# Low parts of the weights: GpSimd's columns moved to VectorE, in a two-block network on one core

## The chip, the cores and the metric

One core of a Trainium2 chip runs the whole program. The metric is the device time of one execution in microseconds (us). TensorE's matrix rows are called PE here, its weight loads PEld, VectorE DVE, ScalarE ACT, GpSimd POOL, and the engine that issues the transfers SP.

## The reference

A sequence of 256 positions with 1024 channels goes through two blocks, each two layers deep. Cut to what matters:

```
first block, twice:   x += 0.5 * swiglu(rms(x), w_gu, w_down)          # 1024 -> 2*2816 -> 1024
                      x += hybrid_mixer(rms(x))     # gMLP branch, attention over selected keys, gates
                      x += 0.5 * swiglu(rms(x), ...)
x = rms(x)
second block, twice:  x += rms(hybrid_mixer_2(rms(x)))   # gated delta rule, dilated attention
                      x += rms(conv_glu_ffn(rms(x)))     # 1024 -> 2*2816, 3-tap conv, gelu*val, -> 1024
```

All of it is float32. Nearly all arithmetic is products of activations with weight matrices.

## The kernel before

TensorE reads its operands in a reduced float32 form (`R32`), so each float32 operand is cut into a high part (`hi`) and a low part (`lo = value - hi`), and each product is made of three matmuls: hi*hi, lo*hi and hi*lo (`mm3_steps`, L254 to L273).

The activations are cut once per stage. The weights come as pieces of mostly 128 x 1024 numbers (512 KB), and each piece is cut when it is needed: SP loads it into a `wraw` buffer (4 of them), ACT copies it to `whi` (4 buffers, the copy's line is L185), and a subtraction makes `wlo` (4 buffers, line L202 whatever the engine). A `wraw` buffer comes free when both copies are made, `whi` and `wlo` when TensorE has read them. This is `parts` (L233), called by `piece`.

The subtraction is divided by columns: VectorE takes the first ones, GpSimd the last `pool_cols`, which is 384 of a piece (640 for VectorE of a piece of 1024, 384 of 768, 128 of 512). In the mixer of the second block a list `plan` gives a number of its own per piece: there `FULL = 34` of the pieces go to GpSimd whole, the four pieces ahead of them half and half. The first piece of the program goes to VectorE whole.

The stages in their order in time: feed-forward 1 to 205 us, mixer 1 to 380, feed-forward to 580, the same three again to 1155, then the second block: mixer 2 (1155 to 1364), gated feed-forward `conv_glu` (to 1580), and both again (mixer 2 to 1785, `conv_glu` to the end). Feed-forward stages run over 22 pairs of pieces (up projection), then over 8 output chunks of three pieces (down projection).

One step of `conv_glu`'s up projection, for one of 22 pairs: two pieces give 48 matmuls; VectorE multiplies the result by the norm row (`t`), ACT and VectorE run the three-tap convolution (`y`: one ACT instruction and two VectorE ones for each half), ACT applies the gelu (`s`), VectorE multiplies (`p`), ACT rounds it to the high part of `hid`, GpSimd makes the low part of `hid`.

In mixer 2 the delta rule is a long dependent chain of small operations. Its start is `rates` on VectorE: from `bt` over `xa`, `spe`, `spz` and `sps` to `dg`, with the convolution of the keys (`kT`) woven in by hand. The order on TensorE is written by hand there too: `pump` puts a fixed amount of other matmuls (pieces of the input projection) where TensorE would wait for the chain.

The order of the instructions of each engine is otherwise set by a scheduler when the program is built, from its own model of their durations; each engine then runs its list strictly in order.

Of the kernel before, what the change touches and what calls it, by code (L numbers as in the profile page):

```python
# [10 lines left out]
OP = mybir.AluOpType  # L11
# [8 lines left out]
D = 1024  # L20
# [5 lines left out]
NEG = -1.0e30  # L26
TAKEN = -3.0e38
BANKS = {"mm": 3, "sm": 5}
FIRST_COLS = 384
POOL_COLS = 384  # L30
FULL = 34
X_ENG = ((ACT, ACT), (ACT, ACT))
XT_ENG = ((ACT, ACT), (ACT, ACT))
WARM = (0, 5, 3)
# [56 lines left out]
class Kernel:  # L91
# [9 lines left out]
    def run(self, stages=None):  # L101
        nc, I, cp = self.nc, self.I, self.cp
        stages = stages or STAGES
        first = [s for s in stages if s[0] not in ("final", "mixer2", "glu")]
        vec1 = self.load(cp, [P, 8 + 2 * V1], I["vec1"], "vec1")
        self.x, self.ahead = [], []
        self.before = self.latest = self.ready = self.later = None
        self.plan, self.made, self.queue, self.far = [], [], [], 0
        self.pool_cols = FIRST_COLS
        for d in range(KD):  # L110
            n = self.new_x()
            nc.sync.dma_start(n, I["x"][d])
            self.x.append(n)
            if d == 1 and stages[0] == ("ffn1", 0):
                self.ahead.append(self.raw(I["ffn1_gu"][0][0, 0], D, 2))
        if self.ahead:
            self.made.append(self.parts(None, D, 0, step=D // 2))
            self.ahead.append(self.raw(I["ffn1_gu"][0][0, 1], D))
            idle = self.sp.tile([P, T], F32, name="sq", bufs=5)
            nc.vector.memset(idle, 0.0)  # L120
            self.warm(10, idle)
        self.ident = self.load(cp, [P, P], I["ident"], "ident")
        self.ones = cp.tile([P, 1], F32, name="ones")
        nc.vector.memset(self.ones, 1.0)
        self.mhalf = cp.tile([P, 16], F32, name="mhalf")
        nc.vector.memset(self.mhalf, -0.5)
        with Pool(self.tc, name="const1", bufs=1) as cp:
            con = self.vec2 = None
            for n, (kind, l) in enumerate(first):
                if n == 1:  # L130
                    self.second_constants()
                v = vec1[:, 8 + V1 * l:8 + V1 * (l + 1)]
                if kind == "mixer1":
                    if con is None:
                        con = {n: self.load(cp, list(I[n].shape), I[n], n)
                               for n in ("cos1", "sin1", "causal0", "causal1")}
                        self.cos1, self.sin1 = con["cos1"], con["sin1"]
                        self.causal = [con["causal0"], con["causal1"]]
                    self.mixer1(l, v)
                else:  # L140
                    g = V_FFN1 if kind == "ffn1" else V_FFN2
                    self.swiglu(v[:, g:g + 8], I[kind + "_gu"][l], I[kind + "_down"][l])
        if self.vec2 is None:
            self.second_constants()
        self.pool_cols = POOL_COLS
        with Pool(self.tc, name="const2", bufs=1) as cp:
            con = {n: self.load(cp, list(I[n].shape), I[n], n)
                   for n in ("cos2", "sin2", "dil0", "dil1", "cum", "whole", "levels", "ident2")}
            self.cos2, self.sin2 = con["cos2"], con["sin2"]
            self.dilated = [con["dil0"], con["dil1"]]  # L150
            self.cum, self.whole, self.levels = con["cum"], con["whole"], con["levels"]
            self.ident2 = con["ident2"]
            rest = stages[len(first):]
            for n, (kind, l) in enumerate(rest):
                v = self.vec2[:, V2 * l:V2 * (l + 1)]
                g = None
                if n + 1 < len(rest):
                    c = V2 * rest[n + 1][1] + (V_PRE if rest[n + 1][0] == "mixer2" else V_PREF)
                    g = self.vec2[:, c:c + KD]
                if kind == "final":  # L160
                    self.between(vec1[:, :KD], g)
                elif kind == "mixer2":
                    self.mixer2(l, v, g)
                else:
                    self.conv_glu(v, I["up2"][l], I["down2"][l], g)
        for d in range(KD):
            nc.sync.dma_start(self.out[d], self.x[d])
# [52 lines left out]
            self.nc.sync.dma_start(raw[:, c:c + step], src[:, c:c + step])  # L220
        return raw

    def piece(self, src, n, pool_cols=None):

        if self.plan or self.made:
            while self.plan and len(self.made) < 3:
                self.made.append(self.parts(*self.plan.pop(0)))
            for p in self.plan[len(self.ahead):self.far]:
                self.ahead.append(self.raw(p[0], p[1]))
            return self.made.pop(0)  # L230
        return self.parts(src, n, pool_cols)

    def parts(self, src, n, pool_cols=None, tiles=None, step=None):  # L233
        nc = self.nc
        raw = self.ahead.pop(0) if self.ahead else self.raw(src, n)
        if tiles is None:
            hi = self.wp.tile([P, n], R32, name="whi", tag="whi", bufs=4)
            lo = self.wp.tile([P, n], R32, name="wlo", tag="wlo", bufs=4)
        else:
            hi, lo = tiles  # L240
        hf = hi.bitcast(F32)
        step = step or n
        for a in range(0, n, step):
            e = a + step
            self.act(hi[:, a:e], raw[:, a:e])
            c = e - min(step, self.pool_cols if pool_cols is None else pool_cols)
            if c > a:
                self.tt(lo[:, a:c], raw[:, a:c], hf[:, a:c], OP.subtract)
            if c < e:
                self.tt(lo[:, c:e], raw[:, c:e], hf[:, c:e], OP.subtract, nc.gpsimd)  # L250
        return hi, lo

    def mm3(self, ps, w, hs, start=True, stop=True, M=P):
# [312 lines left out]
    def token_layout(self, src, hs, parts=4):  # L566

        ps = [self.bank([P, 512]) for _ in range(2)]
        for _ in self.token_steps(ps, src, hs, parts):
            pass  # L570
        return ps

    def token_steps(self, ps, src, hs, parts=4):
        mm = self.nc.tensor.matmul
        per = KD // parts
        for q in range(parts):
            hi, lo = self.piece(src[q], per * 512)
            for i in range(per):
                k = per * q + i
                w = slice(512 * i, 512 * i + 512)  # L580
                for b in range(2):
                    t = slice(P * b, P * b + P)
                    mm(ps[b], hs[k][:, 0, t], hi[:, w], start=k == 0, stop=False)
                    mm(ps[b], hs[k][:, 1, t], hi[:, w], start=False, stop=False)
                    mm(ps[b], hs[k][:, 0, t], lo[:, w], start=False, stop=k == KD - 1)
                    yield 0.65
# [279 lines left out]
    def mixer2(self, l, vec, following):  # L866
        nc, I = self.nc, self.I
        hs, column = self.scaled(vec[:, V_PRE:V_PRE + 8])
        w = I["w_in2_a"][l]
        wo = I["w_out2"][l]  # L870
        half = lambda m, i: (wo[m, :, 512 * i:512 * i + 512], 512)
        first = {"q": 0, "v": 8, "z": 12, "Q": 16, "K": 20}
        self.plan = [(w[i], D, 512) for i in range(4, 8)]
        for c in ORDER:
            if c == "V":
                self.plan += [(I["w_in2_v"][l, i], D) for i in range(4)]
            else:
                self.plan += [(w[first[c] + i], D, 512 if c in "qvz" else None) for i in range(2)]
                first[c] += 2
        self.plan = [p if n < 4 or n >= 4 + FULL else p[:2] + (p[1],) for n, p in enumerate(self.plan)]  # L880
        self.plan += [half(m, 0) for m in range(KD)]
        with Pool(self.tc, name="mix2", bufs=1) as mp, self.tc.manual_schedule(engines={PE}):

# [70 lines left out]
            for i in range(2):  # L954
                t = mp.tile([P, T], F32, name=f"pm2s{i}")
# [72 lines left out]
            ob, wob = [], []  # L1028

            def delta_part():  # L1030
                for m in range(KD):
                    w = self.piece(None, 0)

                    t = [mp.tile([P, 512], R32, name=n, tag="big", bufs=16) for n in ("obh", "obl")]
                    wob.append(self.parts(*half(m, 1), None, t))
                    yield from self.mm3_steps(part(m), w, oa, m % 2 == 0, False, shared=True)

            def attention_part(m, i):
# [12 lines left out]
            for j, bank in enumerate(ps):  # L1051
# [7 lines left out]
                elif j == 1:  # L1059
                    n = mp.tile([P, 2, T], F32, name="ssum2", tag="as", bufs=3)  # L1060
                    self.tt(n, last, sq, OP.add, nc.gpsimd)
                    a = self.sp.tile([P, T], F32, name="ssum", bufs=3)
                    self.tt(a, n[:, 0, :], n[:, 1, :], OP.add, nc.gpsimd)
                    acc.append(a)
                elif j == 2:
                    a = self.sp.tile([P, T], F32, name="ssum", bufs=3)
# [4 lines left out]
                for i in range(2):  # L1071
                    m = 2 * j + i
# [464 lines left out]
```

## Time and profile before

| | |
|---|---|
| runs | 2001.97 us median of 3 (1999.31 to 2010.21) |
| profiled execution | 2004.46 us, span of its core 2002.8 us |
| PE busy | 1894.3 us (95%) |
| DVE busy | 1321.7 us (66%) |
| POOL busy | 1217.8 us (61%) |
| ACT busy | 988.0 us (49%) |

A span is the time from the first to the last instruction in the trace; the profiled execution's own time is 1.7 us longer. Busy time of an engine is the time in which an instruction of it is under way, so an instruction that has started and stands still counts as busy.

### The profile page before, as it was taken

How to read it: one execution, taken by the hardware profiler on the slowest of the kernel's cores; microseconds unless marked ns; L12 is line 12 of the kernel's file. 1: busy time of each engine (PE TensorE's matmuls, PEld its weight loads, DVE VectorE, ACT ScalarE, POOL GpSimd, SP SyncE). 2: the span in 40 equal slices, each digit the busy share in tenths (PEclk: the TensorE clock that was granted, in tenths of full speed). 3: DMA queues.
4: the chain of work that ended last, by engine and by line, in shares of the span. 5: the costliest groups of instructions: out<-in, count | busy, mean ns of one | idle time of the engine just before them, and what ended most of it. 6: DMA issues, size and time to landing. Idle time of an engine off the chain costs nothing. (4 is left out here: it accounts for less than half of the span.)

```text
span 2002.8 us, 40107 instructions
## 1 busy us (share of the span) xinstructions
PE 1894.3 (95%) x15468; PEld 1822.9 (91%) x15468; DVE 1321.7 (66%) x2270; ACT 988.0 (49%) x1698; POOL 1217.8 (61%) x957
## 2 busy tenths in 40 slices
PE   9999999899999999999999978999899979999988
PEld 8999889899999999899999977879888978789888
DVE  7665685866657755966776567457884484559862
ACT  5444436444445544455445534455554445455553
POOL 5556475655565665665566757565556767555555
PEclk9999999999999999999899989999999989999999
DMA  7566554555656666555566633142555332235553
GB/s 233 187 183 187 182 162 130 187 171 188 184 185 198 193 183 192 170 165 154 169 197 187 193 117 116 57 147 88 166 158 174 126 121 92 68 113 169 165 164 114
DMA packets 102511, 317.17 MB, mean 158 GB/s; under 512 B 13360, under 2 KB 20912, under 8 KB 102320
## 3 DMA queue, kind: packets, MB, share of 16 engines
q1 hardware_dynamic: 102320, 314.61, 50.1%
q8 instruction: 121, 1.98, 0.4%
q14 instruction: 70, 0.57, 0.1%
HBM read 309.58 MB, written 1.05 MB: 155 GB/s over the span
## 5 line engine op out<-in xcount | busy, mean ns | idle before, releaser
L202 POOL TENSOR_TENSOR wlo<-wraw,whi 128x384 fp32r<-128x384 f32 (+1 forms) x609 | 931.0, 1532 | 490.0 <-ACT whi L185 487.3
L263 PE MATMUL mm<-h,whi 128*128 128x256 f32 x6048 | 1085.4, 282 | 18.2 <-DVE h L374 5.2
L263 PEld LDWEIGHTS mm<-h,whi 128*128 128x128 f32 x6048 | 931.9, 190 | 29.4 <-issue 12.1
L185 ACT ACTIVATE whi<-wraw 128x1024 fp32r<-128x1024 f32 (+2 forms) x611 | 611.0, 1003 | 421.2 <-PE mm L263 125.5
L263 PE MATMUL mm<-h,wlo 128*128 128x256 f32 (+1 forms) x3024 | 731.5, 282 | 30.5 <-DVE wlo L202 24.4
L202 DVE TENSOR_TENSOR wlo<-wraw,whi 128x640 fp32r<-128x640 f32 (+3 forms) x563 | 487.8, 867 | 333.8 <-ACT whi L185 332.2
L263 PEld LDWEIGHTS mm<-h,wlo 128*128 128x128 f32 (+1 forms) x3024 | 574.8, 190 | 38.6 <-DVE wlo L202 31.6
L263 PE MATMUL mm<-hid,whi 128*128 128x256 f32 x2112 | 378.9, 282 | 6.9 <-ACT hid L185 6.1
L263 PEld LDWEIGHTS mm<-hid,whi 128*128 128x128 f32 x2112 | 326.4, 190 | 7.7 <-ACT hid L185 6.5
L263 PE MATMUL mm<-hid,wlo 128*128 128x256 f32 x1056 | 257.3, 281 | 2.9 <-DVE wlo L202 2.9
L263 PEld LDWEIGHTS mm<-hid,wlo 128*128 128x128 f32 x1056 | 199.5, 189 | 4.1 <-DVE wlo L202 4.1
L185 ACT ACTIVATE hid<-p 128x256 fp32r<-128x256 f32 x132 | 55.1, 418 | 182.9 <-DVE p L202 182.8
L205 DVE SCALAR_TENSOR_TENSOR y<-t,vec,y 128x254 f32<-128x254 f32 (+1 forms) x176 | 135.8, 828 | 0.0
L202 DVE TENSOR_TENSOR p<-s,t 128x256 f32<-128x256 f32 x88 | 103.4, 1175 | 2.2 <-ACT s L185 2.2
L202 DVE TENSOR_TENSOR t<-mm,rb 128x512 f32<-128x512 f32 x132 | 90.5, 686 | 20.4 <-PE mm L263 12.2
L202 POOL TENSOR_TENSOR hid<-p,hid 128x256 fp32r<-128x256 f32 x44 | 34.7, 789 | 88.3 <-ACT hid L185 88.3
L202 DVE TENSOR_TENSOR hid<-p,hid 128x256 fp32r<-128x256 f32 x88 | 40.7, 463 | 40.2 <-ACT hid L185 40.2
L202 POOL TENSOR_TENSOR ssum<-ssum,sq 128x256 f32<-128x256 f32 x50 | 49.0, 981 | 12.1 <-ACT sq L185 11.1
L185 ACT ACTIVATE s<-y 128x256 f32<-128x256 f32 x44 | 18.4, 417 | 69.1 <-DVE y L205 68.9
L263 PE MATMUL mm<-zh,whi 128*128 128x256 f32 x256 | 46.6, 283 | 4.6 <-DVE gate L202 1.8
L205 DVE SCALAR_TENSOR_TENSOR h<-x,vec,h 128x256 fp32r<-128x256 f32 x72 | 45.8, 644 | 6.2 <-ACT h L185 5.1
L185 ACT ACTIVATE y<-t,vec 128x256 f32<-128x256 f32 x88 | 47.5, 589 | 1.7 <-DVE t L202 1.7
(296 smaller groups left out, 2038.4 us busy)
## 6 DMA issues: line engine op xcount, KB each, us to landing
wraw<-ffn_gu_in SPq DMA_DIRECT2D x175, 512.0 KB
wraw<-w_in_a_in SPq DMA_DIRECT2D x112, 512.0 KB
wraw<-up_in SPq DMA_DIRECT2D x88, 512.0 KB
wraw<-ffn_down_in SPq DMA_DIRECT2D x64, 512.0 KB
wraw<-down_in SPq DMA_DIRECT2D x32, 512.0 KB
wraw<-ffn_down_in SPq DMA_DIRECT2D x32, 384.0 KB
wraw<-w_in_v_in SPq DMA_DIRECT2D x16, 512.0 KB
wraw<-w_out_in SPq DMA_DIRECT2D x16, 512.0 KB
```

The costliest lines, as they stand in the source:

```text
L185: return self.nc.scalar.activation(out, in_, func, **k)
L202: return (eng or self.nc.vector).tensor_tensor(out, a, b, op=op)
L205: return self.nc.vector.scalar_tensor_tensor(out, a, s, b, op0=op0, op1=op1)
L263: mm = lambda a, b, **f: self.nc.tensor.matmul(ps, a, b, skip_group_check=shared, **f)
```

## The change

VectorE makes the low part of every piece alone, in one subtraction of all its columns, and the numbers that divided the columns are gone. GpSimd keeps its other work (the low parts of `hid` and of other activations, sums of squares, rotations). In all, 609 subtractions of `wlo` and 16 of `obl` (the second halves of the output weights in mixer 2, the same operation under another name) leave GpSimd.

```diff
-FIRST_COLS = 384
-POOL_COLS = 384
-FULL = 34
...
-            self.made.append(self.parts(None, D, 0, step=D // 2))
+            self.made.append(self.parts(None, D, step=D // 2))
...
-    def parts(self, src, n, pool_cols=None, tiles=None, step=None):
-        nc = self.nc
+    def parts(self, src, n, tiles=None, step=None):
         raw = self.ahead.pop(0) if self.ahead else self.raw(src, n)
...
         for a in range(0, n, step):
             e = a + step
             self.act(hi[:, a:e], raw[:, a:e])
-            c = e - min(step, self.pool_cols if pool_cols is None else pool_cols)
-            if c > a:
-                self.tt(lo[:, a:c], raw[:, a:c], hf[:, a:c], OP.subtract)
-            if c < e:
-                self.tt(lo[:, c:e], raw[:, c:e], hf[:, c:e], OP.subtract, nc.gpsimd)
+            self.tt(lo[:, a:e], raw[:, a:e], hf[:, a:e], OP.subtract)
         return hi, lo
...
-        self.plan = [(w[i], D, 512) for i in range(4, 8)]
+        self.plan = [(w[i], D) for i in range(4, 8)]
...
-        self.plan = [p if n < 4 or n >= 4 + FULL else p[:2] + (p[1],) for n, p in enumerate(self.plan)]
```

The scheduler orders the program anew. Two places show it. The first is ScalarE in the steady part of `conv_glu`'s up projection, one step of the loop; before:

```order
L185 ACTIVATE whi<-wraw 128x1024
L185 ACTIVATE y<-t,vec_2479 128x256 x2
L185 ACTIVATE whi<-wraw 128x1024
L185 ACTIVATE s<-y 128x256
L185 ACTIVATE hid<-p 128x256
```

and with the change (the lines of the file are five lower here):

```order
L180 ACTIVATE whi<-wraw 128x1024
L180 ACTIVATE s<-y 128x256
L180 ACTIVATE whi<-wraw 128x1024
L180 ACTIVATE hid<-p 128x256
L180 ACTIVATE y<-t,vec_2412 128x256 x2
```

One of the two copies of a step stood behind `hid` and ahead of the next `y`; now both copies stand ahead of `hid`. VectorE's order in the same loop is as before (`t`, `wlo`, four `y`, `wlo`, `p`), with 1024 columns in each `wlo` in place of 640.

The second place is VectorE in the chain of rates at the start of the first mixer 2. Before:

```order
L202 TENSOR_TENSOR ct<-mm,rb 128x512
L1139 TENSOR_SCALAR spz<-spe 128x8
L1141 RECIPROCAL spz<-spz 128x8
L205 SCALAR_TENSOR_TENSOR kT<-ct,vec_2479,kT 128x255
L202 TENSOR_TENSOR spz<-spz,spe 128x8
L202 TENSOR_TENSOR spz_14984<-spz 128x8
L205 SCALAR_TENSOR_TENSOR kT<-ct,vec_2479,kT 128x255
L1149 TENSOR_SCALAR sps<-spz_14984 128x8
```

and with the change:

```order
L197 TENSOR_TENSOR ct<-mm,rb 128x512
L197 TENSOR_TENSOR wlo<-wraw,whi 128x1024
L1128 TENSOR_SCALAR spz<-spe 128x8
L197 TENSOR_TENSOR wlo<-wraw,whi 128x1024
L1130 RECIPROCAL spz<-spz 128x8
L200 SCALAR_TENSOR_TENSOR kT<-ct,vec_2412,kT 128x255
L197 TENSOR_TENSOR wlo<-wraw,whi 128x1024
L197 TENSOR_TENSOR spz<-spz,spe 128x8
L197 TENSOR_TENSOR wlo<-wraw,whi 128x1024
L197 TENSOR_TENSOR spz_14579<-spz 128x8
L200 SCALAR_TENSOR_TENSOR kT<-ct,vec_2412,kT 128x255
L1138 TENSOR_SCALAR sps<-spz_14579 128x8
```

Four subtractions of whole pieces stand here between the chain's operations; a fifth stands directly ahead of `bt`, where the chain begins, and a sixth ahead of its end at `dg`. Before, no `wlo` of VectorE stood in the chain. The order on TensorE is the same as before but for a few rows.

## Rows read from the trace of the kernel before

**Rows 1.** The page: busy us of each engine (share of the span), instructions.

```profile
PE 1894.3 (95%) x15468; PEld 1822.9 (91%) x15468; DVE 1321.7 (66%) x2270; ACT 988.0 (49%) x1698; POOL 1217.8 (61%) x957
```

**Rows 2.** Windows: PE, PEld, DVE, ACT, POOL busy us (instructions), granted clock, DMA share, GB/s.

```profile
50.00:150.00 100.00, 100.00 (x851) 100.00 (x850) 68.11 (x89) 48.37 (x70) 57.45 (x37) 1.00 0.59 185
600.00:700.00 100.00, 100.00 (x885) 100.00 (x884) 73.24 (x94) 50.37 (x75) 60.19 (x38) 1.00 0.61 194
1410.00:1500.00 90.00, 80.92 (x673) 78.14 (x672) 78.28 (x113) 51.97 (x85) 51.28 (x43) 1.00 0.51 163
```

**Rows 3.** The page's costliest groups: busy us, mean ns, idle before and releaser.

```profile
L202 POOL TENSOR_TENSOR wlo<-wraw,whi 128x384 fp32r<-128x384 f32 (+1 forms) x609 | 931.0, 1532 | 490.0 <-ACT whi L185 487.3
L202 DVE TENSOR_TENSOR wlo<-wraw,whi 128x640 fp32r<-128x640 f32 (+3 forms) x563 | 487.8, 867 | 333.8 <-ACT whi L185 332.2
```

**Rows 4.** Timeline of VectorE, one step of `conv_glu`: start, duration in us.

```profile
1440.84 0.83 DVE L202 TENSOR_TENSOR wlo<-wraw,whi 128x640 fp32r<-128x640 f32 x1 [0.84 <-ACT whi L185]
1441.59 3.19 DVE L205 SCALAR_TENSOR_TENSOR y<-t,vec,y 128x255 f32<-128x255 f32 x4
1444.70 0.81 DVE L202 TENSOR_TENSOR wlo<-wraw,whi 128x640 fp32r<-128x640 f32 x1
1445.44 0.41 DVE L202 TENSOR_TENSOR p<-s,y 128x256 f32<-128x256 f32 x1
1445.77 0.68 DVE L202 TENSOR_TENSOR t<-mm,rb 128x512 f32<-128x512 f32 x1
1447.29 0.83 DVE L202 TENSOR_TENSOR wlo<-wraw,whi 128x640 fp32r<-128x640 f32 x1 [0.84 <-ACT whi L185]
```

**Rows 5.** Timeline of GpSimd in the same step.

```profile
1440.89 1.67 POOL L202 TENSOR_TENSOR wlo<-wraw,whi 128x384 fp32r<-128x384 f32 x1 [0.21 <-ACT whi L185]
...
1446.38 0.74 POOL L202 TENSOR_TENSOR hid<-p,hid 128x256 fp32r<-128x256 f32 x1 [2.27 <-ACT hid L185]
```

**Rows 6.** Tile `y`: duration ns least/median/most, first and last start.

```profile
L205 DVE SCALAR_TENSOR_TENSOR y<-t,vec,y x176: 468/474/1254, 1381.5 to 1934.1; 128x255 f32<-128x255 f32 x88, 128x254 f32<-128x254 f32 x88
```

**Rows 7.** Timeline of VectorE at the program's start: a subtraction of 512 columns.

```profile
5.55 0.69 DVE L202 TENSOR_TENSOR wlo<-wraw,whi 128x512 fp32r<-128x512 f32 x1
```

**Rows 8.** Waits of TensorE in both `conv_glu`: us in total, times, longest.

```profile
PE mm L263 <- DVE wlo L202: 10.5, 16, 0.7
...
PE mm L263 <- DVE wlo L202: 10.6, 17, 0.7
PE mm L263 <- ACT hid L185: 3.1, 1, 3.1
```

**Rows 9.** Timeline of VectorE in the chain of rates, first mixer 2.

```profile
1169.24 1.41 DVE L202 TENSOR_TENSOR bt<-bt 128x16 f32<-128x16 f32 x1
...
1182.64 2.30 DVE L1149 TENSOR_SCALAR sps<-spz 128x8 f32<-128x8 f32 x1
1184.97 0.17 DVE L205 SCALAR_TENSOR_TENSOR sps<-sps,spz 128x8 f32<-128x8 f32 x1
...
1188.34 0.16 DVE L205 SCALAR_TENSOR_TENSOR dg<-sps,ea 128x8 f32<-128x8 f32 x1
```

**Rows 10.** Timeline of GpSimd beside it.

```profile
1172.87 12.04 POOL L202 TENSOR_TENSOR wlo<-wraw,whi 128x1024 fp32r<-128x1024 f32 x5
```

**Rows 11.** Waits of TensorE in the two mixers 2.

```profile
PE sm L1171 <- DVE dg L205: 9.8, 1, 9.8
...
PE mm L263 <- POOL wlo L202: 2.6, 2, 2.1
...
PE sm L1171 <- DVE dg L205: 7.5, 1, 7.5
...
PE mm L263 <- POOL wlo L202: 3.4, 3, 2.1
```

**Rows 12.** VectorE's groups by shape, key selection of both mixers 1 (240 to 285, 800 to 850).

```profile
L202 DVE TENSOR_TENSOR wlo<-wraw,whi 128x640 fp32r<-128x640 f32 x12 | 13.7, 1143 | 0.0
...
L202 DVE TENSOR_TENSOR wlo<-wraw,whi 128x640 fp32r<-128x640 f32 x16 | 17.7, 1105 | 2.5 <-ACT whi L185 2.5
```

More of the change, by code (lines that the diff above doesn't have):

```diff
@@ L108, in run @@
         self.plan, self.made, self.queue, self.far = [], [], [], 0
-        self.pool_cols = FIRST_COLS
         for d in range(KD):
@@ L144, in run @@
             self.second_constants()
-        self.pool_cols = POOL_COLS
         with Pool(self.tc, name="const2", bufs=1) as cp:
@@ L221, in raw, with piece @@
         return raw
-    def piece(self, src, n, pool_cols=None):
+    def piece(self, src, n):
         if self.plan or self.made:
@@ L230, in piece @@
             return self.made.pop(0)
-        return self.parts(src, n, pool_cols)
-    def parts(self, src, n, pool_cols=None, tiles=None, step=None):
-        nc = self.nc
+        return self.parts(src, n)
+    def parts(self, src, n, tiles=None, step=None):
         raw = self.ahead.pop(0) if self.ahead else self.raw(src, n)
@@ L877, in mixer2 @@
             else:
-                self.plan += [(w[first[c] + i], D, 512 if c in "qvz" else None) for i in range(2)]
+                self.plan += [(w[first[c] + i], D) for i in range(2)]
                 first[c] += 2
-        self.plan = [p if n < 4 or n >= 4 + FULL else p[:2] + (p[1],) for n, p in enumerate(self.plan)]
         self.plan += [half(m, 0) for m in range(KD)]
@@ L1034, in delta_part @@
                     t = [mp.tile([P, 512], R32, name=n, tag="big", bufs=16) for n in ("obh", "obl")]
-                    wob.append(self.parts(*half(m, 1), None, t))
+                    wob.append(self.parts(*half(m, 1), t))
                     yield from self.mm3_steps(part(m), w, oa, m % 2 == 0, False, shared=True)
```

## The prediction

> **What bounds the kernel now.** I read the page's engine shares first: TensorE is busy 95% of the span, VectorE 66%, GpSimd 61% [rows 1]. A gain can come only from what TensorE waits for, or from its own pace. So next come the windows. In the feed-forward stages TensorE is busy all of 100 us in both windows shown; what VectorE and GpSimd do there is hidden, at any speed that keeps up. In `conv_glu` TensorE is busy 80.92 of 90 us and VectorE 78.28: there VectorE's chain sets the pace [rows 2]. The list of waits names the places: 16 and 17 waits for `wlo` in the two `conv_glu`, 10.5 and 10.6 us, with a last one of 3.1 us for `hid` [rows 8], and in the mixers 2 single long waits for the chain of rates, 9.8 and 7.5 us, and 2.6 and 3.4 us for GpSimd's `wlo` [rows 11].
>
> The central reading is the timeline of one `conv_glu` step, from one marked `wlo` to the next: 1440.84 to 1447.29, 6.45 us [rows 4]. VectorE's four `y` take 3.11 us from their start to the next instruction's. The same shapes take 468 ns at the least [rows 6], about 0.39 from start to start if the overlap is that of `wlo` (0.81 long, next start after 0.74 [rows 4]). Four are 1.56, so 1.55 us are lost. In that time GpSimd runs its `wlo`, one of which takes 1.67 us [rows 5]. Over the program GpSimd's `wlo` have a mean of 1532 ns for mostly 384 columns [rows 3]. The two engines stand in each other's way: while one subtracts, the other's instruction that has begun does not finish.
>
> The chain of rates shows it more sharply. An operation on 128x8 numbers takes 0.17 us at 1184.97 and 2.30 at 1182.64 [rows 9]; the slow ones end when GpSimd's run of five whole pieces (12.04 us) ends [rows 10].
>
> **What the Trainium skill says.** Its page "SBUF — State Buffer", section "Who interferes with whom", has it that a VectorE instruction with two SBUF inputs and a GpSimd instruction that reads SBUF exclude each other for the whole instruction. The rows agree: 0.17 against 2.30 us. By that rule, splitting a subtraction between the two gains nothing, as in the sum below. Its page "Perfetto Trace Analysis", section "Optimizing Scalar/DVE Operations", speaks the other way, that work of a saturated VectorE may be given to GpSimd (with the warning that the shared port may spoil it); what would follow from that is the first rival.
>
> **The change, part by part.** Price of one piece: 512 columns take 0.69 us [rows 7], 640 take 0.83 [rows 4], so 0.14 for 128 and 0.42 for the 384 that GpSimd had. A whole piece: 0.83 + 0.42 = 1.25 us, and 0.74 + 0.42 = 1.16 from start to start.
>
> *`conv_glu`.* VectorE's step becomes two pieces 2.32, four `y` 1.56, `p` 0.33, `t` 0.60 (0.68 less the overlap): 4.81 us. The 0.84 us of waiting for ACT's copy ahead of one `wlo` [rows 4] should go, since that copy now stands ahead of `hid` in ACT's order and is made in the step before. Against VectorE remains GpSimd's `hid`, 0.74 us [rows 5], which I add fully as the bad end: 5.55. TensorE's 48 matmuls take 48/885 to 48/851 of 100 us [rows 2], 5.42 to 5.64. So the step comes to about 5.55, whoever leads, 0.90 less than 6.45. With the 33 waits counted [rows 8]: 30 us. The last wait (3.1 in one layer; the other layer shows the same, so I count two) comes from VectorE being steps behind when the matmuls of the up projection end; when it keeps up, most goes: 4 of 6. Together -34, ends -10 (step at 6.15) and -40 (step at 5.42, both last waits gone).
>
> *Mixer 2, rates.* In the first layer six operations of this chain are stretched, from `bt` at 1.41 to `sps` at 2.30 [rows 9]; they sum to 13.2 us where their unhindered shapes sum to 1.6 (four at 0.17, two `kT` at 0.48): 11.6 freed. Six `wlo` now stand in the chain or directly ahead of it, 6 x 1.16 = 7.0 added. Net -4.6, of a wait of 9.8. For the second layer I scale by the waits: 4.6 x 7.5/9.8 = 3.5. The waits for GpSimd's own `wlo`, 6.0 in all [rows 11], halve, as 1.25 us is about half of the 2.4 that one of the five takes (12.04/5): -3. Together -11; ends 0 and -23 (all four waits). The rest of that mixer's chain I leave at zero: VectorE gets whole pieces there, but loses stretched operations as in the rates, and `pump` covers both.
>
> *Mixer 1.* During key selection VectorE is never idle before a `wlo` in the first layer, so its time counts. But its 640 columns take 1.143 us there and 1.105 in the second [rows 12], stretched already. Unhindered whole pieces at 1.25 cost 12 x 0.11 + 16 x 0.15 = 3.7 us more: +4. Ends: +12 (28 x 0.42, if nothing is given back) and -3.
>
> *Feed-forward stages.* Zero: what VectorE does between two steps costs 0.84 us more per pair of pieces, in steps where it is busy about 70 of 100 us [rows 2]; TensorE covers it. If that cover went, 0.84 for each of 88 pairs is +74, but VectorE would first have to fill the free 30%. TensorE's own pace does differ between such stretches, 851 against 885 instructions in 100 us [rows 2], and I see nothing in the change that picks one; moving one up projection of some 120 us from one pace to the other is 5 us. I put that into the range.
>
> Sum: -34 - 11 + 4 = -41. On the profiled execution's 2004.5 that is 1963; the runs' median of 2002.0 is 2.5 lower, so I forecast **1960 us**.
>
> **The rivals.**
>
> *First: VectorE is simply full.* If the stretched `y` were VectorE's own work, 78.28 busy of 90 us plus 28 pieces x 0.42 gives 90.0: the step would stay at 6.45 and `conv_glu` give nothing. For it: the share of 87%. Against it: the 468 ns of `y` [rows 6]. Also in this rival: GpSimd's `hid` and ACT's copies make new waits that use up what is freed. Then only mixers count: 2004.5 - 11 + 4 - 2.5 = 1995.
>
> *Second, slower: pieces in the delta rule's way.* VectorE works in order. A `wlo` placed ahead of a chain operation holds the chain until ACT's copy is there, and that copy may wait for a buffer that TensorE frees only behind its wait for the chain. Place: mixer 2, behind the rates. In the new order six whole pieces stand in the rates and 18 behind them in each mixer 2. If all 36 of the two layers fall on the path, 36 x 1.16 = 42 us are added, and the 11 of the rates are lost: 1960 + 53 = 2013. It ends above 2012, slower by 0.5%, only from (52 - 11)/1.16 = 35 of the 36 pieces on. For it: before, VectorE had hardly a `wlo` there. Against it: whole pieces on GpSimd held up the same operations for 2.3 us each [rows 9].
>
> That the change does nothing is excluded, as no `wlo` is left in GpSimd's order.
>
> **How the numbers follow.** A measurement of this kernel tells about 0.5%, 10 us, from no change. The forecast's own case, 0.80, spans 1942 (mixer waits all gone, -12, and `conv_glu` at its end, -6) to 1985 (step at 5.9: +12; mixer 1 at its end: +8; pace +5). The first rival has 0.14, the second 0.06. The range is 1942 to 1990: it leaves out 0.04 of the forecast's case, 0.10 of the first rival and the second whole. Faster by over 0.5% (below 1992): 0.80 + 0.04 = 0.84; within: 0.10; slower: 0.06.
>
> **What would show it.** In the profile after, `y` at about 0.47 us throughout, the `conv_glu` step near 5.5 us, and the waits of TensorE for `wlo` there gone; whole pieces at 1.25 us on VectorE; the chain from `bt` to `dg` near 14.5 us in place of 19.1; the operations on 128x8 at 0.17. I am wrong if `y` stays stretched (then GpSimd was not what held it), if the step stays above 6 us, or if TensorE's waits in mixer 2 name VectorE's `wlo` or a chain operation queued behind one.

## The result and the profile after

| | before | after |
|---|---|---|
| median, run side by side | 2003.73 us (4 runs) | 1938.01 us (4 runs, 1936.34 to 1949.23) |
| ratio | | 0.9681, 95% interval 0.9635 to 0.9728 |
| profiled execution | 2004.46 us | 1939.03 us (span 1937.3) |

The kernel became 3.2% faster, 22 us more than forecast and 4 us below the low end of the range. The profiled executions differ by 65.4 us, the terms of the sum make 41.

The page's engine shares, which answer to [rows 1], and its group for the low parts, which answers to [rows 3]; GpSimd has no such group any more:

```profile
PE 1874.7 (97%) x15468; PEld 1815.3 (94%) x15468; DVE 1340.8 (69%) x2318; ACT 996.2 (51%) x1698; POOL 323.6 (17%) x332
...
L197 DVE TENSOR_TENSOR wlo<-wraw,whi 128x1024 fp32r<-128x1024 f32 (+2 forms) x611 | 715.1, 1172 | 368.2 <-ACT whi L180 366.3
```

GpSimd gave up 894 us of busy time, and VectorE's rose by only 19, though its `wlo` cost 227 us more (715.1 for 487.8): some 208 us in which its instructions had stood still are gone. The windows, columns as in [rows 2]:

```profile
50.00:150.00 100.00, 100.00 (x851) 100.00 (x850) 66.82 (x89) 47.77 (x71) 0.00 (x0) 1.00 0.63 185
...
1410.00:1500.00 90.00, 90.00 (x786) 90.00 (x785) 73.78 (x106) 57.55 (x90) 21.00 (x16) 1.00 0.63 191
```

The feed-forward stages are as they were. In `conv_glu` TensorE is now busy all 90 us in place of 80.92, and runs 786 matmuls where it ran 673. The timeline of VectorE in one step there, which answers to [rows 4], and the whole row of tile `y`, which answers to [rows 6]:

```profile
1442.00 1.23 DVE L197 TENSOR_TENSOR wlo<-wraw,whi 128x1024 fp32r<-128x1024 f32 x1
1443.14 2.15 DVE L200 SCALAR_TENSOR_TENSOR y<-t,vec,y 128x255 f32<-128x255 f32 x4
1445.21 1.22 DVE L197 TENSOR_TENSOR wlo<-wraw,whi 128x1024 fp32r<-128x1024 f32 x1
1446.34 0.42 DVE L197 TENSOR_TENSOR p<-s,y 128x256 f32<-128x256 f32 x1
1446.68 0.68 DVE L197 TENSOR_TENSOR t<-mm,rb 128x512 f32<-128x512 f32 x1
1447.44 1.23 DVE L197 TENSOR_TENSOR wlo<-wraw,whi 128x1024 fp32r<-128x1024 f32 x1
```

```profile
L200 DVE SCALAR_TENSOR_TENSOR y<-t,vec,y x176: 468/474/975, 1362.3 to 1867.8; 128x255 f32<-128x255 f32 x88, 128x254 f32<-128x254 f32 x88
```

The step takes 5.44 us in place of 6.45 (5.65 in the second `conv_glu`). The four `y` take 2.07 us to the next instruction's start in place of 3.11. The one `y` that is still long lies beside GpSimd's `hid`, the only thing GpSimd has left in the step (its timeline, as [rows 5]):

```profile
1442.35 1.48 POOL L197 TENSOR_TENSOR hid<-p,hid 128x256 fp32r<-128x256 f32 x1 [3.96 <-ACT hid L180]
```

It too is hindered: 1.48 us in place of its 0.74 [rows 5], and VectorE's `wlo` at 1442.00 had begun first.

**Where the 65 us came from.** TensorE runs the same 15468 matmuls in nearly the same order in both kernels, so a matmul can be found in both traces by its number. The table takes the first matmul of each stretch and of the next one and gives the difference of the two distances: what the stretch became shorter by. One profile stands on each side, so a stretch carries the scatter of single executions too.

| stretch (two of each) | shorter by, us | in the sum |
|---|---|---|
| `conv_glu`, up projections | 14.6 + 11.6 | 30 |
| `conv_glu`, down projections | 8.0 + 6.6 | 4 |
| seams: end of mixer 1 into the next feed-forward | 10.0 + 10.0 | none |
| mixers 2 | 3.0 + 3.7 | 11 |
| mixers 1 up to the seam | 0.6 - 3.4 | -4 |
| feed-forward behind mixer 1, up projections | 4.1 + 0.0 | 0 |
| all else | -3.3 | 0 |
| sum | 65.5 | 41 |

### The profile page after: what moved, and what is told of

Read it like the earlier page. It is cut to its first block, busy times and chain, and to the rows that moved or that the text cites. A ratio compares the mean times of both kernels' runs of the same rounds, so it can differ in the third digit from the quotient of the medians.

```text
span 1937.3 us, 38949 instructions
## 1 busy us (share of the span) xinstructions
PE 1874.7 (97%) x15468; PEld 1815.3 (94%) x15468; DVE 1340.8 (69%) x2318; ACT 996.2 (51%) x1698; POOL 323.6 (17%) x332
## 4 chain that ended last, share of the span: by engine, by line
PE 78%; DVE 11%; ACT 3%; issue 3%; DMA 2%; POOL 2%; SPq 1%; DVEq 0%; ACTq 0%; POOLq 0%
PE mm L253 68%; DVE wlo L197 3%; ACT whi L180 1%; PE sm L617 1%; SPq L593 1%; PE sm L326 1%; DMA rm2s<-rm 1%; DMA wraw<-w_out_in 1%; PE sm L650 1%; DVE score L200 1%; PE sm L1261 1%; DMA pm2s<-rm 1%; POOL x L197 1%; PE sm L636 1%; PE sm L1377 1%
## 5 line engine op out<-in xcount | busy, mean ns | idle before, releaser
L197 DVE TENSOR_TENSOR wlo<-wraw,whi 128x1024 fp32r<-128x1024 f32 (+2 forms) x611 | 715.1, 1172 | 368.2 <-ACT whi L180 366.3
L253 PE MATMUL mm<-hid,whi 128*128 128x256 f32 x2112 | 374.1, 279 | 0.0
L197 POOL TENSOR_TENSOR ssum<-sq 128x256 f32<-128x256 f32 x19 | 23.4, 1233 | 653.5 <-ACT sq L180 653.5
L197 POOL TENSOR_TENSOR hid<-p,hid 128x256 fp32r<-128x256 f32 x44 | 62.8, 1428 | 183.4 <-ACT hid L180 154.6
L200 DVE SCALAR_TENSOR_TENSOR y<-t,vec,y 128x255 f32<-128x255 f32 (+1 forms) x176 | 92.5, 578 | 0.0
L197 POOL TENSOR_TENSOR ssum<-ssum,sq 128x256 f32<-128x256 f32 x50 | 55.0, 1101 | 204.1 <-ACT sq L180 178.7
L197 POOL TENSOR_TENSOR as<-as,ast 128x512 f32<-128x512 f32 (+1 forms) x32 | 26.4, 829 | 121.4 <-DVE ast L625 92.2
L253 PEld LDWEIGHTS mm<-zh,whi 128*128 128x128 f32 x256 | 39.0, 188 | 2.0 <-ACT zh L180 1.8
L573 PE MATMUL mm<-whi,h 128*128 128x512 f32 x96 | 38.9, 406 | 0.0
```

Source lines behind the costliest of these rows:

```text
L197: return (eng or self.nc.vector).tensor_tensor(out, a, b, op=op)
L200: return self.nc.vector.scalar_tensor_tensor(out, a, s, b, op0=op0, op1=op1)
L253: mm = lambda a, b, **f: self.nc.tensor.matmul(ps, a, b, skip_group_check=shared, **f)
```

## The experiments

The theory: VectorE's instructions with two SBUF inputs and GpSimd's reads of SBUF shut each other out, and the gain is the end of that. The rivals, each as the whole cause: the scheduler's new order of ScalarE's copies gives the gain; or GpSimd's part was only late, so that TensorE waited for it; or any busy GpSimd slows VectorE. A second run of the changed kernel (below) had a median of 1936.4, so differences are taken from 1937.

**Restoring the division in one part.** Four kernels bring GpSimd's columns back in one part of the program:

```diff
-            self.tt(lo[:, a:e], raw[:, a:e], hf[:, a:e], OP.subtract)
+            c = e - min(step, self.cols if cols is None else cols)
+            if c > a:
+                self.tt(lo[:, a:c], raw[:, a:c], hf[:, a:c], OP.subtract)
+            if c < e:
+                self.tt(lo[:, c:e], raw[:, c:e], hf[:, c:e], OP.subtract, self.nc.gpsimd)
```

They set `self.cols` to 384 in `conv_glu`; from the pieces of `w_pa` to the fourth pair of the next feed-forward; in mixer 2, with the old numbers of `plan`; and in `swiglu`. Elsewhere it is 0.

> The changed kernel, with GpSimd's 384 columns of each piece restored in the two gated feed-forwards conv_glu alone. Exclusion (my theory): the stretched y come back, the step goes from 5.44 to about 6.45 us, and the time goes from 1938 to 1972 (+34, the term of my sum) or 1979 (+41, the difference of the two traces over these stages). Rival 'the gain lies in the new order elsewhere': 1938 to 1945.

Measured: 1982.9 us (1976.8 to 1988.1), +46. By the table's method the up projections lose 14.3 and 11.5 us and the down projections 6.8 and 6.7, 39.3 in place of 40.8. This profile is 48.3 us longer than the changed kernel's; nearly all of the rest lies in the two feed-forwards behind mixer 1, which this kernel leaves alone, 4.1 us in each: the pace of TensorE that is told below. The step is back at 6.44, with the copy's wait and the stretched `y` of [rows 4]:

```profile
1471.34 0.83 DVE L198 TENSOR_TENSOR wlo<-wraw,whi 128x640 fp32r<-128x640 f32 x1 [0.90 <-ACT whi L181]
1472.09 3.19 DVE L201 SCALAR_TENSOR_TENSOR y<-t,vec,y 128x255 f32<-128x255 f32 x4
...
1477.78 0.82 DVE L198 TENSOR_TENSOR wlo<-wraw,whi 128x640 fp32r<-128x640 f32 x1 [0.84 <-ACT whi L181]
```

This run brings back two things at once, the reads and ScalarE's old order of copies. The old step of 6.45 holds a wait of 0.84 for the copy; without it VectorE's instructions, stretched `y` and all, take 5.61. Early in each stage one step still has a copy ahead of `hid` and no wait; from one `t` to the next it takes 5.75 in the first `conv_glu` and 5.66 in the second. The first:

```profile
1380.28 0.68 DVE L198 TENSOR_TENSOR t<-mm,rb 128x512 f32<-128x512 f32 x1
...
1382.13 2.91 DVE L201 SCALAR_TENSOR_TENSOR y<-t,vec,y 128x255 f32<-128x255 f32 x4
...
1386.03 0.68 DVE L198 TENSOR_TENSOR t<-mm,rb 128x512 f32<-128x512 f32 x1
```

The changed kernel's steps are 5.44 and 5.65, both TensorE's pace. The other half alone, whole pieces and free `y` in the old order, comes to an estimated 6.45 + 0.78 (two longer `wlo`) - 1.04 (`y`) = 6.19. So by these rows most of what a step gains hangs on the new place of the copy, and no run has the one without the other.

TensorE's waits in the first `conv_glu` show what ends the up projection, and a window where the down projection begins shows the granted clock (the last figure but two):

```profile
PE mm L258 <- DVE wlo L198: 10.4, 17, 0.8
PE mm L258 <- ACT hid L181: 3.0, 1, 3.0
```

```profile
1500.00:1508.00 8.00, 5.69 (x35) 5.70 (x36) 3.78 (x7) 4.33 (x7) 4.38 (x5) 0.79 0.57 175
```

Ahead of the wait of 3.0 us, where the down projection opens, stand four shorter ones of 2.1 in all, three of them for `wlo`. Behind it the clock is granted at 0.79 in the mean of this window, part of it at 1.2 GHz in place of 2.4. In the changed kernel the same place has neither waits nor a lower clock. Together that is why the end of the stage is worth 7 us and not the 3.0 of the one wait.

> The changed kernel, with GpSimd's columns restored only where mixer 1 ends and the next feed-forward begins: the pieces of w_pa, w_pb and w_out and the first four pairs of the feed-forward behind it, in both layers. If the 20 us that the two traces differ by at these two seams come from GpSimd's columns there: about 1958 (1952 to 1962). If they come from the order of the scheduler or from the clock and only happen to lie there: 1938 within 5.

Measured: 1965.0 us (1962.8 to 1966.6), +28; the seams themselves lose 12.2 and 7.4, 19.6 in place of 20.0. Two feed-forward stages behind them ran at the slower pace, 4.1 and 4.2. So the 20 us are GpSimd's columns. VectorE at the first seam in this kernel, then in the changed one:

```profile
371.39 1.23 DVE L198 TENSOR_TENSOR gate<-gate 128x256 f32<-128x256 f32 x1
372.54 1.61 DVE L198 TENSOR_TENSOR wlo<-wraw,whi 128x640 fp32r<-128x640 f32 x1
...
374.41 1.36 DVE L198 TENSOR_TENSOR wlo<-wraw,whi 128x640 fp32r<-128x640 f32 x1
```

```profile
370.58 0.42 DVE L197 TENSOR_TENSOR gate<-gate 128x256 f32<-128x256 f32 x1
370.92 1.22 DVE L197 TENSOR_TENSOR wlo<-wraw,whi 128x1024 fp32r<-128x1024 f32 x1
```

GpSimd beside the first of these two:

```profile
369.54 3.93 POOL L198 TENSOR_TENSOR wlo<-wraw,whi 128x384 fp32r<-128x384 f32 x3 [2.16 <-ACT whi L181]
```

640 columns take 1.61 and 1.36 us where 1024 take 1.22 with GpSimd quiet, and the `gate` of one shape 1.23 in place of 0.42. A window across the seam's second half, in this kernel and in the changed one, shows what this does to TensorE (second figure: its busy time; the clock stands last but two):

```profile
396.00:406.00 10.00, 6.52 (x39) 5.96 (x38) 8.36 (x13) 3.16 (x5) 4.39 (x5) 0.79 0.54 164
```

```profile
396.00:406.00 10.00, 9.93 (x88) 9.85 (x87) 5.74 (x9) 4.51 (x6) 0.71 (x1) 1.00 0.50 150
```

39 matmuls in place of 88: TensorE waits, and where it goes on the clock is granted at 0.79 in the mean. The loss has two parts, waits and a lower clock behind them. That the columns cause it is shown by this run; that they do it by holding VectorE is read from the stretched rows, since no run adds idle reads at the seams as the one below does in `conv_glu`.

> The changed kernel, with the kernel before's division restored in the two mixers 2 alone (34 whole pieces to GpSimd, four half and half, 384 columns of the rest). My sum has 11 us for these stages, the difference of the two traces over them only 6 (2.4 and 3.7). Forecast's term: 1949; the traces: 1944; rival 'the pieces on VectorE hold the chains up as much as GpSimd did': 1938 or below. Six us are little against the scatter of single runs of 6 us each way, so the alignment of the traces in the mixers counts more than the median.

Measured: 1946.7 us (1943.6 to 1948.8), +10; the mixers lose 5.8 and 1.7, 7.5 in place of 6.7. In the seven other profiles that leave mixers 2 alone their sum is 1.3 us less to 2.7 more than in the changed kernel's first one, so the 7.5 stands clear of that scatter. The forecast's 11 was too high by 4. TensorE's waits in the first mixer 2, here and in the changed kernel, say why:

```profile
PE sm L1168 <- DVE dg L201: 9.8, 1, 9.8
PE sm L1261 <- POOL LT L1241: 5.9, 1, 5.9
PE mm L258 <- POOL wlo L198: 2.4, 2, 2.1
```

```profile
PE sm L1160 <- DVE dg L200: 4.9, 1, 4.9
PE mm L253 <- DVE wlo L197: 4.1, 1, 4.1
PE sm L636 <- POOL as L197: 3.6, 2, 3.5
```

The wait for `dg` halves, those for GpSimd's `LT` and `wlo` go, and two new ones of 4.1 and 3.6 take up over half of what was freed.

> The changed kernel, with GpSimd's 384 columns restored in the six feed-forward stages of the first block, whose pairs leave VectorE some 30 of 100 us free. My sum has nothing for these stages: within 5 of 1938, and each difference of the traces along a stage a steady one of 0.7 us in 150 matmuls (the two paces of TensorE), not waits. At the seam into the second feed-forward the first pairs are divided again, so up to 10 of the 20 us there may return: 1938 to 1953. Rival 'the cover is thinner than it looks and waits return': over 1953.

The stages are four, not the six of this text. Measured: 1943.4 us (1938.2 to 1947.0), +6. The seams lose 1.1 and 1.3 us; behind them the feed-forward stages have the times of the changed kernel or differ by one step of the pace. The cover holds, as forecast.

**Reads and clears by an idle GpSimd.** The next kernels leave the change as it is and give GpSimd work that nobody needs in both `conv_glu`, with its own tile `idle`. Reads:

```diff
             self.tt(lo[:, a:e], raw[:, a:e], hf[:, a:e], OP.subtract)
+        if self.idle:
+            z = self.idle.tile([P, 384], F32, name="idle", bufs=2)
+            self.tt(z, hf[:, n - 384:], hf[:, n - 384:], OP.subtract, self.nc.gpsimd)
```

> The changed kernel, and in both conv_glu GpSimd subtracts, for each piece, 384 columns of whi from themselves into a tile that nobody reads. VectorE still makes the whole low part, and no instruction waits for GpSimd's result. Exclusion: VectorE's instructions with two SBUF inputs (two wlo 2.32, y 1.56, p 0.33 per step) and GpSimd's reads (two of about 1 us and hid 0.74) can't overlap, so the step goes from 5.44 to between 6.9 and 7.3 us and the time to between 2000 and 2030. Rival 'GpSimd's part was late, nothing else': nobody waits, so 1938 within 5. Rival 'the order of ScalarE's copies': that order is as in the changed kernel, so 1938 within 5.

Measured: 1969.8 us (1962.0 to 1973.9), +33. By the table's method 27.6 of this profile's 30.4 lie in the two `conv_glu`. Both rivals expected nothing and fall as the whole cause: ScalarE's copies stand in the order of the changed kernel, and nothing waits for GpSimd's result (two copies wait 2.5 us in all until it has read their buffer). What the run shows is that GpSimd's reads lengthen the step in the new order; it doesn't tell what their end was worth in the old one. My size was wrong, a step of 5.88 us and not 6.9. VectorE, then GpSimd, in one step:

```profile
1475.83 0.68 DVE L198 TENSOR_TENSOR t<-mm,rb 128x512 f32<-128x512 f32 x1
1476.43 1.24 DVE L198 TENSOR_TENSOR wlo<-wraw,whi 128x1024 fp32r<-128x1024 f32 x1
1477.60 2.73 DVE L201 SCALAR_TENSOR_TENSOR y<-t,vec,y 128x255 f32<-128x255 f32 x4
1480.24 1.21 DVE L198 TENSOR_TENSOR wlo<-wraw,whi 128x1024 fp32r<-128x1024 f32 x1
```

```profile
1475.65 0.94 POOL L198 TENSOR_TENSOR idle<-whi 128x384 f32<-128x384 f32 x1 [1.89 <-ACT whi L181]
1476.56 1.73 POOL L198 TENSOR_TENSOR hid<-p,hid 128x256 fp32r<-128x256 f32 x1
1478.73 0.91 POOL L198 TENSOR_TENSOR idle<-whi 128x384 f32<-128x384 f32 x1 [0.45 <-ACT whi L181]
```

I had added up all three GpSimd instructions as lost time. But the first `idle` lies beside `t`, which reads one input from PSUM, and `t` takes the 0.68 us that it takes without it. `hid` is the one that waits while `wlo` runs. Only the four `y` are held, 2.64 us to the next start where 4 x 0.39 = 1.56 are needed: 1.08 us, and 4.81 + 1.08 = 5.89 is the step.

Clears, the first time:

```diff
+        if self.idle:
+            z = self.idle.tile([P, 384], F32, name="idle", bufs=2)
+            for _ in range(3):
+                self.nc.gpsimd.memset(z, 0.0)
+            self.act(self.idle.tile([P, 1], F32, name="seen", bufs=2), z[:, :1])
```

> As the run with reads, but GpSimd writes zeros three times over a tile of 384 columns for each piece (some 0.4 us each, so 1.2 us per piece as the reads took) and reads nothing. A one-column ScalarE copy paces it. Exclusion through reads: 1938 to 1945, y stays at 0.47 us. Rival 'any busy GpSimd slows VectorE': the step goes to 6.9 or more and the time to 2000 or more.

Measured: 1943.6 us (1937.1 to 1949.3). The scheduler let the clears run ahead of the pieces, so that they fill GpSimd without a break to 1450 us and are then used up. A window of that stretch (busy us of PE, PEld, DVE, ACT, POOL):

```profile
1370.00:1440.00 70.00, 70.00 (x597) 70.00 (x596) 67.55 (x104) 54.83 (x128) 66.57 (x149) 1.00 0.59 191
```

GpSimd is busy 66.57 of 70 us and TensorE waits for nothing. The second run with clears spreads them over all steps, since each piece's clears wait for a copy out of its `whi`.

```diff
...
+            self.act(z[:, :1], hf[:, :1])
+            for _ in range(3):
+                self.nc.gpsimd.memset(z, 0.0)
```

> The run with GpSimd's writes once more. In the first one the clears stood in the first slices of each stage, ahead of the steps, and so told nothing. Here each piece's three clears of a 384-column tile wait for a one-column ScalarE copy out of that piece's whi, so that six clears (6 x 0.42 = 2.5 us) lie in every step of both conv_glu, beside VectorE's y and wlo, as the reads did. Exclusion through reads: y takes 0.47 us but for those beside hid, the step stays at TensorE's pace of 5.4 to 5.65, and the time within 6 of 1937. Rival 'any busy GpSimd slows VectorE': y stretched as in the run with reads or more, the step at 5.9 or above, the time at 1965 or above.

One sentence there is wrong: as the window above shows, the clears of the first run did lie beside steps, those of the stage's first half, and told the same. Measured: 1943.1 us (1938.8 to 1950.7). VectorE, then GpSimd:

```profile
1449.61 2.15 DVE L201 SCALAR_TENSOR_TENSOR y<-t,vec,y 128x255 f32<-128x255 f32 x4
1451.68 1.21 DVE L198 TENSOR_TENSOR wlo<-wraw,whi 128x1024 fp32r<-128x1024 f32 x1
```

```profile
1448.82 1.47 POOL L198 TENSOR_TENSOR hid<-p,hid 128x256 fp32r<-128x256 f32 x1 [1.08 <-ACT hid L181]
1450.23 1.36 POOL L246 MEMSET idle<- 128x384 f32 x3
```

The four `y` take 2.07 us to the next start, to the hundredth what they take without the clears, though three clears lie beside them; with reads beside them they took 2.64. So GpSimd's reads hold VectorE, not its work as such. The Trainium skill, "SBUF — State Buffer", section "Who interferes with whom", says the same: a VectorE instruction with two SBUF inputs contends with a GpSimd instruction that reads, not with one that only writes. The two up projections differ from the changed kernel by +2.8 and -2.8, as they do in the second run of the changed kernel that follows.

**The pace, and the rest of GpSimd's work.**

> The changed kernel again, unaltered. If the pace of TensorE in the up projections (113 or 118 ns from matmul to matmul) belongs to the program, each stage shows the pace it had: the first feed-forward slow, the second fast, the up projection of the second conv_glu slow. If it is drawn anew in each execution, some stage changes pace, which is worth 4 to 5 us per up projection, and the time scatters by such steps: 1932 to 1949.

Measured: 1936.4 us (1934.3 to 1940.3). The same program, another draw: both feed-forwards behind mixer 1 took 4.1 and 4.2 us longer in the up projection, the two of `conv_glu` 2.8 longer and 2.8 shorter. A window of the first profile and of this one, TensorE busy without a gap in both:

```profile
420.00:510.00 90.00, 90.00 (x796) 90.00 (x795) 63.07 (x83) 45.53 (x67) 0.00 (x0) 1.00 0.64 192
```

```profile
420.00:510.00 90.00, 90.00 (x767) 90.00 (x766) 60.57 (x80) 43.87 (x64) 0.00 (x0) 1.00 0.62 185
```

The 4.1 us of the table's last row but two are such a draw, not the change. What draws it is not settled.

The next run carries the theory on and takes every two-input operation but the powers from GpSimd:

```diff
-        return (eng or self.nc.vector).tensor_tensor(out, a, b, op=op)
+        return self.nc.vector.tensor_tensor(out, a, b, op=op)
```

> The changed kernel with every other two-input operation of GpSimd given to VectorE as well (low parts of hid, sums of squares, rotations, the scaling of the attention's probabilities, sums of x); GpSimd keeps the powers, the selects by position and the clears. Exclusion carried to its end: VectorE loses no more to GpSimd, at 0.36 us for hid in place of up to 0.6, so the steps stay at TensorE's pace and TensorE's waits for GpSimd's as (7.1) and gv (3.0) change their name or go: 1925 to 1945. Rival 'VectorE becomes the bound in the seams and chains, since work that GpSimd did beside it now stands in its one queue': 1945 to 1965.

Measured: 1944.0 us (1941.5 to 1948.8), against 1936.4 beside it. No gain, and if anything 8 us of loss: the waits for `as` stay and only change their name to ScalarE's (6.3 us), those for `Tf` on VectorE grow from 6.3 to 9.7. So with the columns of the weights gone, taking the rest of GpSimd's reads away is worth nothing more here.

**Filling the waits that are left.** Two numbers of the hand-made order on TensorE were raised: 5.8 to 10.5 us of other matmuls ahead of `dg`, and 1.1 to 2.4 in the attention's first steps.

```diff
-WAIT = {"ba": 5.8, ...
+WAIT = {"ba": 10.5, ...
...
-            self.pump(fill)
+            self.pump(first if n <= deep and first else fill)
...
```

> The changed kernel, with 10.5 instead of 5.8 us of other matmuls put ahead of the delta rule's first wait (for dg) in both mixers 2. VectorE's order up to dg is unaltered by it. If what is left of that wait (10.3 us in all) is a true gap and the pieces for the added matmuls are there in time: TensorE's waits for dg shrink by up to 2 x 4.7 and the time goes to 1929 (1927 to 1933). Rival: those matmuls are missing later in the chain, where a wait opens in their place, or they wait for VectorE's wlo which stand in the same queue as the chain: 1936 to 1942.

> The changed kernel, with 2.4 instead of 1.1 us of other matmuls between the first steps of the attention in both mixers 2, where TensorE waits 3.5 us for as. If the gap is covered: up to 7 us less, 1931 (1930 to 1934). Rival: the matmuls run out and a later step waits: 1938 within 3.

> Both of these together. If both gaps are covered and nothing opens elsewhere: 1922 to 1927. If the first matmuls are missing later: 1930 to 1940.

Measured: 1947.4 (1940.9 to 1949.5), 1940.7 (1935.8 to 1948.1) and 1943.4 (1937.6 to 1954.3), none better than the changed kernel. The waits of the first of the three:

```profile
PE sm L1397 <- POOL do L197: 9.0, 2, 4.5
...
PE sm L1160 <- DVE dg L200: 2.9, 2, 1.6
```

The wait for `dg` falls from 10.3 to 2.9 us, and one for `do` of 9.0 opens at the other end of the chain: the matmuls that fill gaps are a fixed amount. By the table's method the first mixer 2 became 1.5 us shorter and the second 6.8 longer. In mixer 2 a shorter wait is worth less than its length, since another part of the chain takes its place.

## Why the prediction was right, and where it failed

*The mechanism* is real: reads by GpSimd lengthen `y` with nothing else changed (5.88 for 5.44 us a step), clears do not. The first rival, a full VectorE, falls with the step of 5.44 us. What is not shown is the mechanism's share in `conv_glu`: the sum's step takes in the copy's wait of 0.84 as well as the freed `y`, and by the rows of the first run above the copy's new place may have given most of it. The Trainium skill's other page, "Perfetto Trace Analysis", section "Optimizing Scalar/DVE Operations", allows giving GpSimd part of a saturated VectorE's work and warns that between these two it might not help; here the division, with the order that came with it, costs 39 to 41 us in `conv_glu` alone.

One reading is wrong: the 2.30 us that the prediction sets against 0.17 as agreeing with the rule on two inputs belong to an operation with one SBUF input, `sps` at 1182.64. The two-input ones beside GpSimd's whole pieces are `spz` at 1175.47 and 1177.87, 2.37 and 2.29 us. Why the one-input operation stood still too, no run tells.

*The `conv_glu` step*: 5.55 forecast, 5.44 and 5.65 measured; 26.2 for 30. Right. (Four of the 33 waits counted stand in the openings of the down projections; 29 steps of 0.90 make 26.)

*Its last wait*: 4 forecast, 14.6 measured. I sized it by one row of the list of waits, 3.1 us for `hid`. In the kernel before, each layer has four short waits ahead of it, 1.9 us in all and three of them for `wlo`, and behind it a stretch at the lower clock. Counted from the first matmul on `hid`, the two ends lose 8.9 and 7.6 us, of which the waits are 4.9 each; the rest is the clock, and all of it goes. A term of the sum too small by 10.

*Mixers 2*: 11 forecast, 6.7 measured. The chain from `bt` (the one row [rows 9] begins with, now at 1151.53) to `dg` (1164.91) takes 13.4 us, 14.5 forecast (one of the six pieces counted in it stands ahead of `bt`; with five it is 13.3), and its operations on 128x8 their 0.15 to 0.17; the whole pieces stand between them as in the order. VectorE in that chain, as [rows 9]:

```profile
1153.28 1.76 DVE L197 TENSOR_TENSOR wlo<-wraw,whi 128x1024 fp32r<-128x1024 f32 x1
1154.97 0.16 DVE L1128 TENSOR_SCALAR spz<-spe 128x8 f32<-128x8 f32 x1
...
1164.91 0.16 DVE L200 SCALAR_TENSOR_TENSOR dg<-sps,ea 128x8 f32<-128x8 f32 x1
```

Where [rows 10] had five whole pieces on GpSimd, now two short ones run, and one of them stretches the `wlo` at 1153.28:

```profile
1152.53 0.74 POOL L197 TENSOR_TENSOR cosr<-cos,rb 128x256 f32<-128x256 f32 x1 [2.75 <-DVE rb L988]
1153.22 0.75 POOL L197 TENSOR_TENSOR sinr<-sin,rb 128x256 f32<-128x256 f32 x1
```

The step that failed is "the rest of that mixer's chain I leave at zero". Waits of 4.1 for a `wlo` and 3.6 for `as` opened in it:

```profile
1204.34 0.58 PE L253 MATMUL mm<-h,wlo 128*128 128x256 f32 x1 [4.05 <-DVE wlo L197]
```

That `wlo` was the prediction's third sign of being wrong, and the second rival turned round: its copy was made by 1198.55, but it stood behind other operations of that stage on VectorE until 1203.07. The second rival itself, slower than before, did not come.

*Mixers 1*: +4 forecast. The profile has +2.8, a second profile of the same program 3.0 less than before. Within that scatter nothing can be said. The pieces in the key selection take 1.42 us in the first layer, not the 1.25 forecast, beside other GpSimd reads (as [rows 12]):

```profile
L197 DVE TENSOR_TENSOR wlo<-wraw,whi 128x1024 fp32r<-128x1024 f32 x14 | 19.9, 1418 | 0.3 <-ACT whi L180 0.3
```

*Feed-forward*: 0 forecast. Right for the steady stages, by the run that restores them alone.

*The seams*: 20 us that the sum does not have. This is the step that failed most: "the list of waits names the places" was read for `conv_glu` and mixers 2 alone, and the step from mixer 1 into the next feed-forward was in no term. The rows were there in the trace of before, VectorE stretched and TensorE waiting 5.6 us around the first seam, with the clock at 0.69 in the mean of 396 to 406; VectorE there, and that window:

```profile
370.28 1.62 DVE L202 TENSOR_TENSOR wlo<-wraw,whi 128x640 fp32r<-128x640 f32 x1
```

```profile
396.00:406.00 10.00, 6.69 (x34) 6.28 (x33) 6.37 (x10) 1.94 (x4) 3.87 (x5) 0.69 0.51 163
```

With the seams at 20 and the ends at 14.6, in place of 0 and 4, the forecast would have been 1960 - 31 = 1929; with mixers 2 at 6.7, 1934.

## What to carry to other kernels

A subtraction divided between VectorE and GpSimd, both with two SBUF inputs, was no gain in any part of this program that was tried, and it stretched VectorE's other two-input instructions near it. A change that makes the scheduler order the program anew is two changes; to tell them apart takes a run with the one alone. Before such a change is priced, every stretch where TensorE idles should be listed, from the whole span and with its lower-clock stretches, not only the stages that come to mind; the transitions between stages count. In the hand-filled dependent chain here a wait that shrank came back in part elsewhere, so it is priced below its length.

## What the runs showed of the hardware

Continuous 256-column matmuls of the same program run at one of two paces, 796 or 767 in 90 us, 113 or 118 ns from start to start, at a granted clock of 1.00 in both. Between the two profiles of the changed kernel it differs in four of the six up projections and holds through each, where it is worth 4.1 us of about 105; in `conv_glu` it is 4.0 to 4.2, of which the stretch's opening gives 1.2 to 1.4 back. Not all stages change: in all 14 profiles every down projection ran at 118 ns and the up projection of the third feed-forward at 113.

GpSimd's clear of 128x384 takes 0.42 us (0.41 to 0.43 in all 384 of the first run with clears) and neither holds nor is held beside VectorE's `y` and `wlo`; its subtraction of 128x384 takes 0.91 to 0.94 in the step shown, where a VectorE instruction with a PSUM input, or a held one, lies beside it. The hold goes both ways: VectorE's `y` lost 1.08 us in a step, GpSimd's `hid` 0.99.
